# Modulations first in one run, half of their blocks in fp32, tokens in groups of three tiles; residual rows in eight pieces, output stores in halves; two loads of the neighbourhood stage moved

## The chip, the cores and the metric

One core of one Trainium2 chip runs the whole program. The metric is the device time of one execution in microseconds. Five engines work side by side: TensorE (PE; its weight loads, PEld, overlap its products), VectorE (DVE), ScalarE (ACT), GpSimd (POOL) and SyncE (SP), which here does nothing but issue DMAs. Each engine runs its instructions in a fixed order and waits on semaphores for what others make. Transfers issued by one engine stand in its instruction order too: a DMA whose wait isn't met holds up those behind it.

## What is computed

Two layers of a diffusion backbone work on 1024 latent tokens (a grid of 16 rows by 64 columns) and 128 prompt tokens, 1024 features each. Layer 0 mixes tokens by latent attention with 16 heads, layer 1 by neighbourhood attention with 16 heads over the grid. Around both stands the same frame, cut here to what the change touches:

```python
for i in range(DEPTH):                                   # 2
    sh_p, sc_p, g_p = modulation(c_ctx, w_ada[i], b_ada[i])   # split(silu(cond) @ w + b, 3)
    sh_s, sc_s, g_s = modulation(c, w_ada[i], b_ada[i])
    hp = rms_norm(xp, pre_norm_g[i]) * (1.0 + sc_p) + sh_p
    hs = rms_norm(xs, pre_norm_g[i]) * (1.0 + sc_s[:, None]) + sh_s[:, None]
    ...                                                  # op, osm: the mixer and its output projection
    xp = xp + g_p * rms_norm(op, post_norm_g[i])
    xs = xs + g_s[:, None] * rms_norm(osm, post_norm_g[i])
```

All tensors are fp32. The kernel keeps the precision by splitting an operand into two fp32r parts (high: the rounded value, low: the rest) and adding three products of the parts (`mm3`, line 84).

## The kernel before

**Staging.** Tokens come in nine tiles of 128 rows: tiles 0 to 7 latent, tile 8 prompt. Weights come by SP into a ring of raw buffers and are split by ACT (high part, a cast) and DVE or POOL (low part, a subtraction) (`load_w`, `split_to`).

**The opening (lines 162 to 298).** Layer 0 needs two modulation vectors before any token can be built: s = 1 (scale) and s = 0 (shift). For each, `modulation_steps` goes through eight blocks of `w_ada` (128 x 1024, 512 KB): load into one of four raw buffers, split, and four products of 512 columns (two column halves, high and low part) with a stationary operand of four columns: the conditioning vectors' high and low parts. `modulation_cols` then turns the rows into columns by small fp32 products (line 183). The program's order is: modulation 1, load and normalise x tiles 0 to 3, modulation 0, gate weights of head 0, x tiles 4 to 7, build the transposed normalised tokens `hT` for tiles 0 to 3, gate weights of head 1, x tile 8, normalise tiles 4 to 8, build 4 to 7, build 8. `norm_x` works tile by tile: two squares on ACT, then seven small instructions on DVE with a square root on ACT between, and one scaling. `build_ko` transposes a block of columns on PE (line 236), applies scale and shift (even blocks on DVE, odd ones on ACT) and splits. The gates of heads 0 and 1 follow as products over three groups of 384 tokens each (`proj_group`, line 395; `gate`, line 431).

```python
for _ in modulations(0, (1,)): pass
load_x(range(0, 4)); norm_x(range(0, 4))
for _ in modulations(0, (0,)): pass
```

**Order of the work.** A planner orders the instructions of each engine in the opening by their place in the program and by times that it reckons; SP is ordered by it throughout. `tc.issue_after(ins)` puts what is traced in its block behind `ins` on that engine. From the attention loop on, and again from line 1723 to the end, the orders of PE, ACT, DVE and POOL are those written out by hand.

**The neighbourhood stage (lines 1714 to 1811).** 64 units (8 head pairs, 4 column groups, 2 heads) run through a software pipeline, index k from -2 to 63; `NORDER` lists the steps of one k. `pair_proj` projects queries and keys of a head pair; `put_k` writes keys and copies them by DMA to the other half of the partitions (line 1440; `last_k` is the last of these). `windows(p, cg)` loads the values of a column group, five DMAs (lines 1567 and 1570), into one of two buffers, once for two units. `out_load` loads gated rows of an output tile into a raw buffer and notes them for a split; `last_split` does the split that is noted. In one k the step `W` does one piece of the output weights, which also splits what is noted.

**The tail (lines 1812 to 1820).** For each of nine output tiles PE makes 48 products of 512 columns (`out_steps`). `out_norm` loads the tile's residual rows and calls `post_norm`: squares on ACT, scaling by the gate row on DVE (line 1140), inverse root, then per half one `scalar_tensor_tensor` that adds the residual (line 1144), then one store of the whole tile. Because a tile here is 8 grid rows by 16 grid columns, its residual rows come in four DMAs of 32 rows, each two runs of 16 rows in DRAM:

```python
src = [x1_d[4 * rg + q].rearrange("(r c) f -> r c f", c=GW)[:, 16 * cg:16 * cg + 16, :] for q in range(4)]
return [(xr[32 * q:32 * q + 32, :], src[q]) for q in range(4)]
```

The buffers for residual rows and for results (`nq0`, `nq1`) are two each.

Of the kernel before, what the change touches and what calls it, by code (L numbers as in the profile page):

```python
# [3 lines left out]

# [1 line left out]

# [5 lines left out]
F32 = mybir.dt.float32  # L12
F32R = mybir.dt.float32r
AF = mybir.ActivationFunctionType
# [42 lines left out]
def hybrid_step(ctx: ExitStack, tc: tile.TileContext, i, o):  # L57
# [103 lines left out]

    def modulation_steps(l, s, ring):

        mod5 = pg.tile([5, D], F32, tag="mod5", name="mod5", bufs=1)
        dma(mod5[4:5, :], i["b_ada"][l:l + 1, s * D:(s + 1) * D])
        pm = [bank("M"), bank("M")]
        for k in range(NKO):
            w2 = load_w(ring, i["w_ada"][l, k * P:(k + 1) * P, s * D:(s + 1) * D], 2, 4, V,
                        lambda: pg.tile([P, 1024], F32, tag="raw", name="w_raw", bufs=4))
            for n in range(2):  # L170
                for e, w in enumerate(w2):
                    nc.tensor.matmul(pm[n][0:4, :], cs[:, k, :], w[:, n * 512:(n + 1) * 512],
                                     start=k == 0 and e == 0, stop=k == NKO - 1 and e == 1)
# [80 lines left out]
    ph1 = es_h1.enter_context(tc.tile_pool(name="ph1", bufs=1))  # L254
    hT = [ph1.tile([P, NKO, NTOK], F32R, name=f"hT{e}") for e in range(2)]
    pg = es_h1.enter_context(tc.tile_pool(name="pg", bufs=1, reuse_waits="tile"))

    def modulations(l, ss, ring=pg):
        for s in ss:
# [10 lines left out]
    def load_x(ts):  # L270
        with tc.issue_after(last_load[0]):
            for t in ts:
                last_load[0] = dma(xt[t], i["xs"][t * P:(t + 1) * P, :] if t < NLT else i["xp"]).ins

    def norm_x(ts):
        for t in ts:
            r = row_rstd(xpool, halves(xt[t]))
            V.tensor_scalar(xt[t], xt[t], r[:, 0:1], None, ALU.mult)

    for _ in modulations(0, (1,)):  # L280
        pass
    def build_h0(w, t0, n):
        build_h(0, w, lambda ko: xpool.tile([P, 512], F32, tag="htmp", name="htmp", bufs=3), xt[t0:t0 + n],
                lambda e, ko: hT[e][:, ko, t0 * P:(t0 + n) * P])

    load_x(range(0, 4))
    norm_x(range(0, 4))
    for _ in modulations(0, (0,)):
        pass
    gw = [gate_w(0)]  # L290
    load_x(range(4, 8))
    build_h0(0, 0, 4)
    gw.append(gate_w(1))
    load_x([8])
    norm_x(range(4, NT))
    build_h0(0, 4, 4)
    build_h0(1, 8, 1)
    es_x.close()

    es1 = ExitStack()  # L300
# [94 lines left out]
    def proj_group(w, src, g, evac, tag):  # L395

        ps = bank(tag)[:, :384]
        for ko in range(NKO):
            mm3(ps, [w[e][:, ko * P:(ko + 1) * P] for e in range(2)], [src(e, ko, g) for e in range(2)],
                ko == 0, ko == NKO - 1)  # L400
        evac(g, ps)

    def load_head(h, tile_):

        raw, rr = tile_[:, 0:512], None
# [22 lines left out]
        split_to(wv[0], wv[1], raw[:, 384:512])  # L428
        head_wv[h] = wv

    def gate(h, w, tag="S"):
        def evac(g, ps):
            gt = pg.tile([P, 384], F32, tag="gt", name="gt", bufs=3)
            S.activation(gt, ps, AF.Silu)
            dma(gate_d[h][:, g * 384:(g + 1) * 384], gt)
        for g in range(3):
            proj_group(w, lambda e, ko, g: hT[e][:, ko, g * 384:(g + 1) * 384], g, evac, tag)
            yield

    gates = [gate(h, w) for h, w in enumerate(gw)]  # L440
    for _ in zip(*gates):
        pass
    narrow(0)
    for h in range(2, 6):
        for _ in gate(h, gate_w(h)):
# [684 lines left out]
    for _ in rest:  # L1130
        pass

    def post_norm(pool, xr, parts, x_src, gp, dst, *junk_ring):

        for d, sr in x_src(xr):
            dma(d, sr)  # L1136

        def scaled():
            for x, c0, n in parts:
                V.tensor_tensor(dst[:, c0:c0 + n], x, gp[:, c0:c0 + n], ALU.mult)  # L1140
        r = row_rstd(pool, [x for x, _, _ in parts], scaled, *junk_ring)
        for _, c0, n in parts:
            c = slice(c0, c0 + n)
            V.scalar_tensor_tensor(dst[:, c], dst[:, c], r[:, 0:1], xr[:, c], ALU.mult, ALU.add)

    gpt = [t4(f"gpt{w}") for w in range(2)]
    for w in range(2):
# [394 lines left out]
                ko == 0, ko == 7)  # L1542
            yield

    def out_norm(t):
        parts = [(ps, hf * 512, 512) for hf, ps in enumerate(outs[t])]
        cg, rg = t // 2, t % 2

        def x1_rows(xr):
            if t == NLT:  # L1550
                return [(xr, x1_d[8])]
            src = [x1_d[4 * rg + q].rearrange("(r c) f -> r c f", c=GW)[:, 16 * cg:16 * cg + 16, :] for q in range(4)]
            return [(xr[32 * q:32 * q + 32, :], src[q]) for q in range(4)]
        xr, y = [p5.tile([P, NTOK], F32, tag=x, name=f"xy_{x}", bufs=2)[:, 0:D] for x in ("nq0", "nq1")]
        post_norm(p5, xr, parts, x1_rows, gpu[0 if t < NLT else 1], y, ("pf", 5))
        if t < NLT:
            dst = o["ys"].rearrange("(r c) f -> r c f", c=GW)
            dma(dst[8 * rg:8 * rg + 8, 16 * cg:16 * cg + 16, :], y)
        else:
            dma(o["yp"], y)  # L1560

    ogs, outs = {}, {}

# [179 lines left out]
    for k in range(-2, N):  # L1743
# [14 lines left out]
        if k == N - 2:  # L1758
# [8 lines left out]
        for step in NORDER.split():  # L1767
# [15 lines left out]
            elif c == "h":  # L1783
                on(na_hi, k + 1, int(n))
            elif c == "l":
                on(na_lo, k + 1, int(n))
            elif c == "E":
                on(na_values, k)
            elif c in "fg" and k >= 0:
                it = its[k]  # L1790
                na_out(it["po"], it["e"], 256, "fg".index(c))
                if it["e"] == 1 and c == "g":
                    gt = pairs[it["p"]]["gt"]
                    na_gate(it["p"], grid(gt)[:, :, 16 * it["cg"]:16 * it["cg"] + 16],
                            (2 * it["cg"], 2 * it["cg"] + 1), 256)
            elif c == "J":
                for _ in range(int(n) + (k < 0)):
                    next(proj, None)
            elif c == "K" and later:
                later.popleft()()  # L1800
            elif c == "X" and k >= N - 8:
                for _ in range(int(n)):
                    if n_out < 14 or k > N - 2:
                        next(out, None)
                        n_out += 1
            elif c == "W":
                (slow.popleft() if slow else last_split)()
# [116 lines left out]
```

## Time and profile before

| | |
|---|---|
| median of three runs | 2196.53 us (2195.59 to 2197.91) |
| the profiled execution's own time | 2195.93 us |
| its span in the trace | 2194.1 us |
| PE busy | 2016.6 us, 92% of the span |
| DVE, ACT, POOL busy | 1474.7, 1113.5, 850.0 us |
| moved by DMA | 256.49 MB, mean 117 GB/s |

The span runs from the first to the last instruction; the execution's own time has 1.8 us more around it. Times in the trace count from the span's start. A matmul's end is modelled, so a busy PE isn't PE at its peak. The granted clock (PEclk) is a share of 2.4 GHz; 0.5 is 1.2 GHz.

### The profile page before, as it was taken

The page shows a single profiled execution, that of the slowest core. Times are in us where ns is not written, and L with a number is a line of the kernel's source. Part 1 is how long each engine was busy: PE and PEld are TensorE (multiplying, and loading weights), DVE is VectorE, ACT ScalarE, POOL GpSimd, SP SyncE. Part 2 cuts the span into 40 slices and gives each one's busy share as a digit, 9 for nine tenths or more (in the row PEclk, how much of TensorE's full clock was granted, in tenths as well). Part 3 has the DMA queues.
Part 4 walks back from the last instruction along what each step waited for, and adds up shares of the span by engine and source line. Part 5 has one row for each costly group of instructions (what it writes and reads, how often), then busy time and mean ns, then how long its engine had stood idle before and what let it go on. Part 6 is the DMA issues. An engine that isn't in the chain of part 4 may idle for free.

```text
span 2194.1 us, 37839 instructions
## 1 busy us (share of the span) xinstructions
PE 2016.6 (92%) x13166; PEld 1864.7 (85%) x13166; DVE 1474.7 (67%) x3258; ACT 1113.5 (51%) x2582; POOL 850.0 (39%) x843
## 2 busy tenths in 40 slices
PE   6999998989999898889897799999998999998995
PEld 2899998888888888889897688889888999998784
DVE  6723887778888878787887744542215888887742
ACT  7545115555656566656564433343114667666621
POOL 0412215666777667766764500010001333333300
PEclk8999999999999999999999999999999999999898
DMA  7223752212221213121212733335324555566632
GB/s 285 86 79 109 233 168 67 58 45 63 55 65 44 75 34 91 51 77 32 69 40 77 238 125 120 113 106 187 133 104 138 170 179 179 174 186 208 202 123 85
DMA packets 172740, 256.49 MB, mean 117 GB/s; under 512 B 19651, under 2 KB 137187, under 8 KB 172549
## 3 DMA queue, kind: packets, MB, share of 16 engines
q1 hardware_dynamic: 172420, 253.96, 37.2%
q8 instruction: 104, 1.70, 0.3%
q14 instruction: 88, 0.71, 0.1%
q0 software_dynamic: 128, 0.11, 0.0%
HBM read 182.58 MB, written 51.49 MB: 107 GB/s over the span
## 4 chain that ended last, share of the span: by engine, by line
PE 35%; DMA 7%; DVE 4%; ACT 3%; POOL 2%; issue 2%; SPq 1%; DVEq 0%; POOLq 0%; ACTq 0%
PE ps_S L87 14%; PE ps_W L87 8%; DMA xy_nq<-x_d 4%; PE ps_M L87 4%; PE ps_M L1643 2%; PE ps_T L1618 2%; PE ps_S L1591 1%; PE ps_S L1592 1%; POOL sm L796 1%; DMA w_raw<-in_wout 1%; ACT pf L775 1%; DVE og L82 1%; DMA w_raw<-og_d 1%; SPq L1136 1%; DMA nk<-nk 1%
## 5 line engine op out<-in xcount | busy, mean ns | idle before, releaser
L785 DVE TENSOR_TENSOR pT<-pf,pT 128x512 fp32r<-128x512 f32 (+1 forms) x320 | 308.7, 969 | 24.0 <-ACT pT L780 23.9
L796 POOL TENSOR_TENSOR sm<-sm,pf 128x512 f32<-128x512 f32 (+1 forms) x192 | 258.9, 1348 | 15.9 <-ACT pf L775 1.7
L87 PE MATMUL ps_M<-pT,cK 128*128 128x256 f32 x1728 | 259.3, 296 | 1.3 <-DVE pT L785 1.3
L87 PE MATMUL ps_W<-h,w 128*128 128x384 f32 x1152 | 239.5, 347 | 0.0
L87 PEld LDWEIGHTS ps_M<-pT,cK 128*128 128x128 f32 x1728 | 230.9, 198 | 1.9 <-DVE pT L785 1.9
L87 PEld LDWEIGHTS ps_W<-h,w 128*128 128x128 f32 x1152 | 200.3, 190 | 5.7
L717 PE MATMUL ps_S<-qA,cKT 128*128 128x256 f32 x1152 | 190.8, 285 | 5.1 <-ACT pf L775 4.7
L87 PE MATMUL ps_S<-hT,w_hi 128*128 128x384 f32 x720 | 188.3, 339 | 4.8 <-DVE hT L82 3.8
L780 ACT CAST pT<-pf 128x512 fp32r<-128x512 f32 (+1 forms) x320 | 179.8, 591 | 0.0
L717 PEld LDWEIGHTS ps_S<-qA,cKT 128*128 128x128 f32 x1152 | 166.6, 192 | 7.6 <-ACT pf L775 7.0
L1613 POOL TENSOR_SCALAR pf<-pf,li 128x512 f32<-128x512 f32 x128 | 91.0, 711 | 204.1 <-DVE li L1610 178.2
L87 PEld LDWEIGHTS ps_S<-hT,w_hi 128*128 128x128 f32 x720 | 130.6, 189 | 6.8 <-DVE hT L82 4.9
L793 POOL TENSOR_TENSOR sm<-pf 128x512 f32<-128x512 f32 x64 | 88.9, 1389 | 108.8 <-ACT pf L775 108.4
L87 PE MATMUL ps_S<-wo,og 128*128 128x512 f32 x432 | 124.9, 397 | 0.0
L762 ACT CAST q<-ps_M 2x256 fp32r<-2x256 f32 x63 | 22.8, 362 | 197.1 <-PE ps_M L756 193.0
L87 PE MATMUL ps_S<-hT,w_lo 128*128 128x384 f32 x360 | 121.2, 337 | 0.0
L1607 ACT ACTIVATE pf<-pf,nm 128x512 f32<-128x512 f32 x128 | 93.0, 727 | 39.6 <-DVE nm L1604 36.2
L775 ACT ACTIVATE pf<-ps_S 128x512 f32<-128x512 f32 x192 | 108.9, 598 | 0.2 <-PE ps_S L768 0.2
L717 PE MATMUL ps_S<-q,KR 128*128 128x256 f32 x384 | 108.7, 284 | 0.4 <-DMA q<-w_raw 0.4
L82 DVE TENSOR_TENSOR og<-w_raw,og 128x512 fp32r<-128x512 f32 x56 | 57.1, 1042 | 67.9 <-ACT og L148 67.9
L495 ACT COPY qt<-ps_W 128x384 f32<-128x384 f32 (+1 forms) x104 | 47.0, 452 | 101.0 <-PE ps_W L87 92.4
L717 PE MATMUL ps_T<-qA,cKT 128*128 128x256 f32 x576 | 97.3, 284 | 0.0
(363 smaller groups left out, 5053.8 us busy)
## 6 DMA issues: line engine op xcount, KB each, us to landing
w_raw<-in_w_ada SPq DMA_DIRECT2D x48, 512.0 KB
w_raw<-og_d SPq DMA_DIRECT2D x41, 512.0 KB
vw<-vd SPq DMA_DIRECT2D x128, 128.0 KB
bias<-in_bias SPq DMA_DIRECT2D x64, 192.0 KB
q<-rp SPq DMA_DIRECT2D x126, 96.0 KB
gate_d<-gt SPq DMA_DIRECT2D x48, 192.0 KB
w_raw<-in_wgate SPq DMA_DIRECT2D x16, 512.0 KB
gt<-gate_d SPq DMA_DIRECT2D x64, 128.0 KB
```

Source lines behind the costliest of these rows:

```text
L82: eng.tensor_tensor(out, a, b, ALU.subtract)
L87: nc.tensor.matmul(ps, lhs[a], rhs[b], start=first and n == 0, stop=last and n == 2)
L495: (eng.copy if eng is S else eng.tensor_copy)(out, src)
L717: nc.tensor.matmul(ps[:, c:c + 256], k_[:, j, :], q_[:, un["qs"]], start=c == 0 and n == 0, stop=n == 3, skip_group_check=True)
L775: S.activation(pf, un["banks"][b][:, :w], AF.Exp)
L780: S.copy(un["pT"][b][0][:, :pf.shape[1]], pf)
L785: V.tensor_tensor(x[1], pf, x[0].bitcast(F32), ALU.subtract)
L793: G.tensor_tensor(un["sm"], un["pf"][0], pf, ALU.add)
L796: G.tensor_tensor(sm[:, :w], sm[:, :w], pf, ALU.add)
L1607: S.activation(it["pf", rg], it["pf", rg], AF.Exp, bias=it["nm", rg], scale=1.0, accum_out=it["li", rg])
L1613: G.tensor_scalar(it["pf", rg], it["pf", rg], it["li", rg][:, 0:1], 1.0, ALU.mult, ALU.mult)
L1618: nc.tensor.transpose(pt[:, j * P:(j + 1) * P], it["pf", rg][:, j * P:(j + 1) * P], ident)
```

## The change

- Opening: both modulations run one after the other in one loop, s = 1 first; s = 0 uses other PSUM banks (S) than s = 1 (M). Of the eight blocks of each, the odd ones aren't split: the raw fp32 block is multiplied in fp32 by `c0`, a new four-column operand that holds the conditioning vectors themselves and zeros (two products in place of four).
- x tiles 0 to 2 are loaded behind blocks 3 to 5 of the first modulation and normalised as a group; tiles 3 to 5 are loaded behind the gate weights of head 0, tiles 6 to 8 behind those of head 1. `norm_x` does its small instructions once for a group of three.
- For each group of three tiles in turn: normalise (groups 1 and 2), build, and the products of that group for the gates of heads 0 and 1. `proj_group` and `gate` move up in the text for this and stay as they were.
- Neighbourhood stage: the window loads traced at k < 2 are issued behind the last key copy; the first load of gated rows stands at the end of step N-13 in place of the start of step N-12; the immediate split at N-11 is left out.
- Tail: the residual rows of the next tile are loaded before a tile's normalisation is traced, in eight DMAs of 16 rows, each one run in DRAM; the store goes in two column halves, each behind its add; the very last half is issued by ACT.

```diff
@@ modulation_steps
-        pm = [bank("M"), bank("M")]
+        pm = [bank("SM"[s]), bank("SM"[s])]
         for k in range(NKO):
-            w2 = load_w(ring, i["w_ada"][l, k * P:(k + 1) * P, s * D:(s + 1) * D], 2, 4, V,
-                        lambda: pg.tile([P, 1024], F32, tag="raw", name="w_raw", bufs=4))
+            src = i["w_ada"][l, k * P:(k + 1) * P, s * D:(s + 1) * D]
+            new = lambda: pg.tile([P, 1024], F32, tag="raw", name="w_raw", bufs=4)
+            if k % 2:
+                raw = new()
+                last_load[0] = dma(raw, src).ins
+                parts = [(c0[:, k, :], raw)]
+            else:
+                parts = [(cs[:, k, :], w) for w in load_w(ring, src, 2, 4, V, new)]
             for n in range(2):
-                for e, w in enumerate(w2):
-                    nc.tensor.matmul(pm[n][0:4, :], cs[:, k, :], w[:, n * 512:(n + 1) * 512],
-                                     start=k == 0 and e == 0, stop=k == NKO - 1 and e == 1)
+                for e, (c, w) in enumerate(parts):
+                    nc.tensor.matmul(pm[n][0:4, :], c, w[:, n * 512:(n + 1) * 512],
+                                     start=k == 0 and e == 0, stop=k == NKO - 1 and e == len(parts) - 1)
             yield
...
+    c0 = pg.tile([P, NKO, 4], F32, name="c0")
+    V.memset(c0, 0.0)
+    for w in range(2):
+        V.tensor_copy(c0[:, :, 2 * w], cs_f[:, :, 2 * w])
@@ norm_x
     def norm_x(ts):
-        for t in ts:
-            r = row_rstd(xpool, halves(xt[t]))
-            V.tensor_scalar(xt[t], xt[t], r[:, 0:1], None, ALU.mult)
+        ss = xpool.tile([P, 3, 2], F32, tag="ssx", name="ss", bufs=2)
+        for k, t in enumerate(ts):
+            for hf, x in enumerate(halves(xt[t])):
+                junk = xpool.tile([P, 512], F32, tag="ntmp", name="junk", bufs=1)
+                S.activation(junk, x, AF.Square, accum_out=ss[:, k, hf:hf + 1])
+        s1 = xpool.tile([P, 3], F32, tag="ss_3", name="ss_3", bufs=2)
+        V.tensor_reduce(s1, ss, AX.X, ALU.add)
+        V.tensor_scalar(s1, s1, 1.0 / D, EPS, ALU.mult, ALU.add)
+        r = rsqrt(xpool, s1, 3)
+        for k, t in enumerate(ts):
+            V.tensor_scalar(xt[t], xt[t], r[:, k:k + 1], None, ALU.mult)
@@ the opening
-    for _ in modulations(0, (1,)):
-        pass
-    load_x(range(0, 4))
-    norm_x(range(0, 4))
-    for _ in modulations(0, (0,)):
-        pass
+    for n, _ in enumerate(modulations(0, (1, 0))):
+        if n in (3, 4, 5):
+            load_x(n - 3)
+        if n == 5:
+            norm_x(range(0, 3))
     gw = [gate_w(0)]
-    load_x(range(4, 8))
-    build_h0(0, 0, 4)
+    for t in range(3, 6):
+        load_x(t)
     gw.append(gate_w(1))
-    load_x([8])
-    norm_x(range(4, NT))
-    build_h0(0, 4, 4)
-    build_h0(1, 8, 1)
+    for t in range(6, NT):
+        load_x(t)
...
+    gates = [gate(h, w) for h, w in enumerate(gw)]
+    for g in range(3):
+        if g:
+            norm_x(range(3 * g, 3 * g + 3))
+        build_h0(0, 3 * g, 3 if g < 2 else 2)
+        if g == 2:
+            build_h0(1, 8, 1)
+        for x in gates:
+            next(x)
...
-    gates = [gate(h, w) for h, w in enumerate(gw)]
-    for _ in zip(*gates):
-        pass
     narrow(0)
@@ post_norm
-    def post_norm(pool, xr, parts, x_src, gp, dst, *junk_ring):
-        for d, sr in x_src(xr):
+    def post_norm(pool, xr, parts, x_src, gp, dst, *junk_ring, put=None):
+        for d, sr in x_src(xr) if x_src else ():
             dma(d, sr)
...
             V.scalar_tensor_tensor(dst[:, c], dst[:, c], r[:, 0:1], xr[:, c], ALU.mult, ALU.add)
+            if put:
+                put(c)
@@ out_norm
+    def out_x(t):
+        cg, rg = t // 2, t % 2
+        xr = p5.tile([P, NTOK], F32, tag="nq0", name="xy_nq0", bufs=2)[:, 0:D]
+        if t == NLT:
+            dma(xr, x1_d[8])
+            return xr
+        for r in range(8):
+            row = r % 2 * GW + 16 * cg
+            dma(xr[16 * r:16 * r + 16, :], x1_d[4 * rg + r // 2][row:row + 16, :])
+        return xr
-    def out_norm(t):
+    def out_norm(t, xr, last):
...
-        post_norm(p5, xr, parts, x1_rows, gpu[0 if t < NLT else 1], y, ("pf", 5))
-        if t < NLT:
+        y = p5.tile([P, NTOK], F32, tag="nq1", name="xy_nq1", bufs=2)[:, 0:D]
+        def put(c):
             dst = o["ys"].rearrange("(r c) f -> r c f", c=GW)
-            dma(dst[8 * rg:8 * rg + 8, 16 * cg:16 * cg + 16, :], y)
-        else:
-            dma(o["yp"], y)
+            dst = o["yp"][:, c] if t == NLT else dst[8 * rg:8 * rg + 8, 16 * cg:16 * cg + 16, c]
+            (nc.scalar.dma_start if last and c.start else dma)(dst, y[:, c])
+        post_norm(p5, xr, parts, None, gpu[0 if t < NLT else 1], y, "pf", 5, put=put)
@@ the neighbourhood loop
-            it["vw"] = windows(it["p"], it["cg"]) if it["e"] == 0 else its[k]["vw"]
+            with tc.issue_after(last_k[0]) if k < 2 else nullcontext():
+                it["vw"] = windows(it["p"], it["cg"]) if it["e"] == 0 else its[k]["vw"]
-        if k in (N - 12 + 1, N - 3, N - 1):
+        if k in (N - 3, N - 1):
             last_split()
-        if k == N - 12:
-            out_load(order[0], slice(0, 7))
...
+        if k == N - 13:
+            out_load(order[0], slice(0, 7))
@@ the tail
+    xr = out_x(order[0])
     for n, t in enumerate(order):
         for _ in out:
             pass
-        out_norm(t)
+        xr, nxt = (out_x(order[n + 1]) if n + 1 < NT else None), xr
+        out_norm(t, nxt, n + 1 == NT)
```

## Rows read from the trace of the kernel before

**Rows 1.** The page, part 1: busy us (share of the span) and instructions.

```profile
PE 2016.6 (92%) x13166; PEld 1864.7 (85%) x13166; DVE 1474.7 (67%) x3258; ACT 1113.5 (51%) x2582; POOL 850.0 (39%) x843
```

**Rows 2.** Windows: from:to, length, busy us (instructions) of each engine, PEclk, DMA share, GB/s.

```profile
20.00:25.00 5.00, 2.71 (x18) 2.02 (x18) 1.49 (x10) 4.83 (x11) 0.00 (x0) 1.00 1.03 420
...
25.00:30.00 5.00, 1.13 (x3) 0.18 (x4) 4.50 (x21) 4.68 (x14) 0.00 (x0) 0.51 0.40 161
...
43.00:80.00 37.00, 31.18 (x168) 28.43 (x169) 33.13 (x69) 25.76 (x59) 19.45 (x15) 0.86 0.59 191
...
80.00:320.00 240.00, 238.54 (x1377) 232.99 (x1376) 143.38 (x279) 89.56 (x199) 47.30 (x40) 1.00 0.43 134
...
2130.00:2144.00 14.00, 14.00 (x63) 11.45 (x62) 5.03 (x12) 2.53 (x6) 0.00 (x0) 1.00 0.31 114
```

**Rows 3.** Timeline of the opening: start us, us, engine line op [idle before].

```profile
6.97 1.01 PE L172 MATMUL ps_M<-w_hi,cs 128*4 128x512 f32 x2 [6.97 <-ACT w_hi L148]
...
20.40 0.62 PE L172 MATMUL ps_M<-w_lo,cs 128*4 128x512 f32 x2 [0.64 <-DVE w_lo L82]
...
28.63 1.02 PE L172 MATMUL ps_M<-w_hi,cs 128*4 128x512 f32 x2 [5.04 <-ACT w_hi L148]
...
42.18 0.63 PE L172 MATMUL ps_M<-w_lo,cs 128*4 128x512 f32 x2
...
48.56 0.81 DVE L245 TENSOR_SCALAR htmp<-ps_T,acol,shcol 128x512 f32<-128x512 f32 x1
...
80.14 1.03 PE L236 MATMUL ps_T<-ident,x 128*128 128x128 f32 x8
```

**Rows 4.** Line 183's instructions: count, duration ns min/median/max, first and last start.

```profile
L183 PE MATMUL ps_T<-sel,mod x32: 246/246/369, 21.4 to 47.4; 5*128 5x2 f32 x32
```

**Rows 5.** Timeline, entry of the neighbourhood stage.

```profile
1657.11 4.34 SPq L1570 DMA_DIRECT2D vw<-vd  x3
...
1661.56 1.47 SPq L1440 DMA_DIRECT2D nk<-nk  x2
...
1663.91 1.43 DVE L82 TENSOR_TENSOR w<-w_raw,w 128x256 fp32r<-128x256 f32 x4
...
1668.01 0.77 PE L1591 MATMUL ps_S<-nk,nq 128*128 128x512 f32 x1 [5.50 <-DMA nk<-nk]
...
1669.00 7.57 PE L87 MATMUL ps_W<-h,w 128*128 128x384 f32 x30
...
1689.47 1.26 PE L1643 MATMUL ps_M<-pT,vw 128*128 128x256 f32 x10
```

**Rows 6.** Timeline, late in the neighbourhood stage.

```profile
2024.49 1.03 ACT L1514 CAST w<-w_raw 128x512 fp32r<-128x512 f32 x2 [4.58 <-DMA w_raw<-og_d]
...
2027.83 2.37 PE L1618 MATMUL ps_T<-ident,pf 128*128 128x128 f32 x8 [5.04 <-POOL pf L1613]
```

**Rows 7.** Timeline of the tail.

```profile
2087.73 4.38 SPq L1136 DMA_DIRECT2D xy_nq<-x_d  x4
...
2092.13 11.31 PE L87 MATMUL ps_W<-nwo,w 128*128 128x512 f32 x48
...
2095.31 1.42 DVE L1144 SCALAR_TENSOR_TENSOR xy_nq<-xy_nq,rs_y,xy_nq 128x512 f32<-128x512 f32 x2
...
2134.03 9.79 SPq L1136 DMA_DIRECT2D xy_nq<-x_d  x4
...
2136.51 11.31 PE L87 MATMUL ps_W<-nwo,w 128*128 128x512 f32 x48
...
2147.82 8.59 SPq L1136 DMA_DIRECT2D xy_nq<-x_d  x4
...
2163.03 10.95 PE L87 MATMUL ps_W<-nwo,w 128*128 128x512 f32 x46 [0.52 <-DVE w L82]
...
2185.81 1.41 DVE L1144 SCALAR_TENSOR_TENSOR xy_nq<-xy_nq,rs_y,xy_nq 128x512 f32<-128x512 f32 x2 [7.37 <-DMA xy_nq<-x_d]
```

**Rows 8.** Line 229's instructions, columns as in rows 4.

```profile
L229 SPq DMA_DIRECT2D gp_d<-mg x2: 379/379/379, 248.1 to 324.6; - x2
```

More of the change, by code (lines that the diff above doesn't have):

```diff
@@ L2 @@
 from collections import deque, namedtuple
-from contextlib import ExitStack
+from contextlib import ExitStack, nullcontext
 import numpy as np
@@ L268, in hybrid_step, with proj_group, load_x @@
     xt = [xpool.tile([P, D], F32, name=f"x{t}") for t in range(NT)]
-    def load_x(ts):
+    def proj_group(w, src, g, evac, tag):
+        ps = bank(tag)[:, :384]
+        for ko in range(NKO):
+            mm3(ps, [w[e][:, ko * P:(ko + 1) * P] for e in range(2)], [src(e, ko, g) for e in range(2)],
+                ko == 0, ko == NKO - 1)
+        evac(g, ps)
+    def load_x(t):
         with tc.issue_after(last_load[0]):
-            for t in ts:
-                last_load[0] = dma(xt[t], i["xs"][t * P:(t + 1) * P, :] if t < NLT else i["xp"]).ins
+            last_load[0] = dma(xt[t], i["xs"][t * P:(t + 1) * P, :] if t < NLT else i["xp"]).ins
     def norm_x(ts):
-        for t in ts:
-            r = row_rstd(xpool, halves(xt[t]))
-            V.tensor_scalar(xt[t], xt[t], r[:, 0:1], None, ALU.mult)
-    for _ in modulations(0, (1,)):
-        pass
+        ss = xpool.tile([P, 3, 2], F32, tag="ssx", name="ss", bufs=2)
[9 more added lines that the diff above has]
+            V.tensor_scalar(xt[t], xt[t], r[:, k:k + 1], None, ALU.mult)
     def build_h0(w, t0, n):
@@ L284, in build_h0, with gate, evac @@
                 lambda e, ko: hT[e][:, ko, t0 * P:(t0 + n) * P])
-    load_x(range(0, 4))
-    norm_x(range(0, 4))
-    for _ in modulations(0, (0,)):
-        pass
+    for n, _ in enumerate(modulations(0, (1, 0))):
[3 more added lines that the diff above has]
+            norm_x(range(0, 3))
     gw = [gate_w(0)]
-    load_x(range(4, 8))
-    build_h0(0, 0, 4)
+    for t in range(3, 6):
+        load_x(t)
     gw.append(gate_w(1))
-    load_x([8])
-    norm_x(range(4, NT))
-    build_h0(0, 4, 4)
-    build_h0(1, 8, 1)
+    for t in range(6, NT):
+        load_x(t)
+    def gate(h, w, tag="S"):
+        def evac(g, ps):
+            gt = pg.tile([P, 384], F32, tag="gt", name="gt", bufs=3)
+            S.activation(gt, ps, AF.Silu)
+            dma(gate_d[h][:, g * 384:(g + 1) * 384], gt)
+        for g in range(3):
+            proj_group(w, lambda e, ko, g: hT[e][:, ko, g * 384:(g + 1) * 384], g, evac, tag)
+            yield
+    gates = [gate(h, w) for h, w in enumerate(gw)]
+    for g in range(3):
+        if g:
[5 more added lines that the diff above has]
+            next(x)
     es_x.close()
@@ L393, in narrow @@
         put_kr(j, pt[:, 3 * P:4 * P])
[L395 to L401, printed above, removed]
     def load_head(h, tile_):
@@ L429, in split_v @@
         head_wv[h] = wv
[L431 to L438, printed above, removed]
-    gates = [gate(h, w) for h, w in enumerate(gw)]
-    for _ in zip(*gates):
-        pass
     narrow(0)
@@ L1140, in scaled @@
                 V.tensor_tensor(dst[:, c0:c0 + n], x, gp[:, c0:c0 + n], ALU.mult)
-        r = row_rstd(pool, [x for x, _, _ in parts], scaled, *junk_ring)
+        r = row_rstd(pool, [x for x, _, _ in parts], scaled, *([junk_ring] if junk_ring else []))
         for _, c0, n in parts:
@@ L1543, in out_steps @@
             yield
-    def out_norm(t):
+    def out_x(t):
[9 more added lines that the diff above has]
+    def out_norm(t, xr, last):
         parts = [(ps, hf * 512, 512) for hf, ps in enumerate(outs[t])]
         cg, rg = t // 2, t % 2
[L1549 to L1554, printed above, removed]
-        post_norm(p5, xr, parts, x1_rows, gpu[0 if t < NLT else 1], y, ("pf", 5))
-        if t < NLT:
+        y = p5.tile([P, NTOK], F32, tag="nq1", name="xy_nq1", bufs=2)[:, 0:D]
+        def put(c):
             dst = o["ys"].rearrange("(r c) f -> r c f", c=GW)
-            dma(dst[8 * rg:8 * rg + 8, 16 * cg:16 * cg + 16, :], y)
-        else:
-            dma(o["yp"], y)
+            dst = o["yp"][:, c] if t == NLT else dst[8 * rg:8 * rg + 8, 16 * cg:16 * cg + 16, c]
+            (nc.scalar.dma_start if last and c.start else dma)(dst, y[:, c])
+        post_norm(p5, xr, parts, None, gpu[0 if t < NLT else 1], y, "pf", 5, put=put)
     ogs, outs = {}, {}
```

## The prediction

> **What bounds the kernel now.** I read the page's first part first: TensorE (PE) is busy for 92% of the span [rows 1], so PE decides, except in stretches where it stands still. The windows show where that is [rows 2]. From 80 to 320 us PE is busy 238.54 of 240 us at 2.4 GHz, so a stretch of work that starts earlier there also ends earlier. Before it stands an opening in which PE waits: 25 to 30 us holds 1.13 us of PE work, and from 43 to 80 us VectorE (DVE) is the fuller engine, 33.13 of 37 us against PE's 31.18 with a granted clock of 0.86. At the other end, 2130 to 2144 us, PE is full, but the transfers move only 114 GB/s at a DMA share of 0.31, while 420 GB/s were possible at 20 to 25 us.
>
> The timeline of the opening [rows 3] has the two modulations that the first normalised rows need: the first from 6.97 to 21.0 us, the second from 28.63 to 42.8 us. Between them the reader sees 7.6 us without a modulation matmul: ScalarE (ACT) and DVE normalise four row tiles, whose instructions stand ahead of the second modulation's splits. The first build instruction comes at 48.56 us.
>
> At the entry of the neighbourhood stage [rows 5] PE waits 5.50 us, to 1668.01, for key copies that SP issued only at 1661.56, behind three window loads whose issuing took from 1657.11 to 1661.5. Late in that stage [rows 6] a PE wait of 5.04 us follows a ScalarE cast that stood 4.58 us for a load of gated rows. In the tail [rows 7] the output products take 11.1 us a tile ((2136.51 - 2092.13) / 4 groups), but the residual rows come ever later: issuing the four pieces of a tile grows from 4.38 to 9.79 us, and the last add waits 7.37 us and starts at 2185.81. (The chain of waits ends there too: the add, and before it these transfers, tile after tile.)
>
> **The opening.** A block of 512 KB now costs four products of 512 columns: 11.31 us for 48 [rows 7], so 0.232 us each at 2.4 GHz and 0.93 us a block. Half of the blocks (8 of 16) become two fp32 products. Their price isn't in the trace. The low end is the same 0.232 us. The high end comes from fp32 rows: eight transposes of 128 columns take 1.03 us [rows 3], 0.109 us apart, so 0.43 us for 512 columns, and line 183's 16 fp32 products stand as 32 records [rows 4], two for each: 0.87 us. I take 0.87, the nearer kind. A block is then 1.74 us, and PE has 8 x 0.81 = 6.5 us more to do. ACT is spared 8 casts, DVE as many subtractions.
>
> A pair of blocks is thus 2.67 us of PE, 21.4 us for all 16; at today's pace (14.1 us for 8) it would be 28.3 us. With the start at 6.97 the second modulation ends between 28.4 and 35.3 us, if the hole of 7.6 us goes; it goes because both modulations now follow each other in every queue and only six row squares stand among their casts. Later than 42.8 us it ends only if PE stays at 1.2 GHz: 42.7 us of products, end at 49.7. Its first matmuls do run at half speed (two in 1.01 us against 0.62 later). I take 33.5 us, near today's pace, because four raw buffers still carry the blocks and three row tiles are loaded among them: 9.3 us gained.
>
> The Trainium skill (FP8 and Floating Point Precision, section "TensorE Precision Notes") speaks against this half of the change: true FP32 goes through the array in four passes. By that, an estimate of 4 x 0.232 = 0.93 us a product, PE would have 7.4 us more in place of 6.5; no row here times such a product, and the 9.3 us would shrink by at most 0.9.
>
> What is late next: DVE. Three groups of three tiles need as many built columns as two of four and one; the small norm instructions come once for a group and not for a tile, which spares DVE some. The two gates' products start with the first three tiles. I give this 0.7 us and 10 us for the whole opening. Its ends: 7 us lost (PE at 1.2 GHz), 16 us gained (28.4 us and a fuller PE afterwards). The moved x loads (nine, each now behind a weight load on SP) stand before PE's first need, at the cost of ACT and DVE stalls where they don't, inside these ends. The shift is carried by the full PE from 80 us on.
>
> **The two neighbourhood loads.** The windows of the first two units go behind the key copies on SP. The copies are then issued when ACT has written the keys, about 1658.5 us, with no window ahead. But PE can't go on at once: the projection of the next pair needs weight splits that DVE does from 1663.91 on (four in 1.43 us), so the first is there at about 1664.3. PE's 30 products at 1669.00 [rows 5] then come 4.7 us earlier. They took 7.57 us; at 0.232 x 384/512 = 0.174 us each they would take 5.2: the wait had brought the clock down to 1.2 GHz, and I count half of the 2.4 us. Together 5.9 us; ends 0 (DVE late by as much) and 7.9. The windows themselves come later by up to 10 us, and the second ones wait for the next pair's first key copies; the first values product that reads a window stands at 1689.47, and that covers it. Without that cover their landing would be PE's wait.
>
> The load of gated rows moves from the start of one step to the end of the step before. Between the two stand only loads, no compute, and the buffer that it needs comes free at the same split, so the 4.58 us wait stays, in the main. One split that was done at once now goes in halves into free places. I take 1 us, with ends of 1 us lost and 7 us gained (the PE wait of 5.04 us and the slow products behind it gone).
>
> **The tail.** A tile's residual rows come now in four pieces of 32 rows, afterwards in eight of 16 rows, each one run of DRAM. Issuing: the 16-row DMA of the trace, line 229, takes 0.379 us [rows 8], so 3.0 us a tile, under the 11.1 us that PE needs. How fast such a piece lands no row shows. The ends are the full rows of the opening (420 GB/s, 512 KB in 1.25 us) and the 32-row pieces of today (four issued in 9.79 us). I take the fast end: what is slow today isn't the memory (share 0.31, 114 GB/s), and 16 rows of 4 KB have the form of the 128-row loads. The Trainium skill (DMA: Bandwidth & Descriptors, section "Why a DMA increments its semaphore by 16 and not by 1") has a rule for this: a DMA runs on the largest number of engines, up to 16, that divides the outermost size of both its sides. By it today's piece, two runs of DRAM, uses two engines, the new one 16, and the sum is as I make it; the share of 0.31 agrees, no view names the engines.
>
> With the rows in time PE keeps its 11.1 us: groups start at 2147.6 and 2158.7 and end at 2169.8, against 2163.03 + 10.95 = 2174.0 now. The add follows a PE end by 3.2 us where it doesn't wait (2095.31 against 2092.13), so 2173.0 in place of 2185.81: 12.8 us. The last store's second half leaves by ACT's queue behind a first half that is already moving; I take 0.8 us, with ends of 0.5 lost and 1.5 gained, by half of a 256 KB share. The earlier halves cost SP one more issue a tile, beside PE's products. Tail: 13.6 us. If a row piece is late now, it is the load of gated rows; it stands behind 3 us of issuing and has a tile's time.
>
> **Sum.** 10 + 5.9 + 1 + 13.6 = 30.5 us off the profiled execution's 2195.93 us (span 2194.1 and 1.8 around it): 2165.4. The median of the runs, 2196.53, is 0.6 us above it: 2166.
>
> **The rivals.**
> - The opening gains nothing: fp32 products at 1.2 GHz, or ACT and DVE unable to feed PE while they build (33 of 37 us busy speaks for it; fewer splits against). 2166 + 10 = 2176.
> - Some waits go altogether: the stall at 2027.83 too, and the opening gives 16 us. 2166 - 6 - 6 = 2154. For it: the load is traced earlier; against: its buffer isn't free earlier.
> - The row pieces stay as slow as today's, so the change doesn't do what it says there: the tail keeps all but the 0.8 us of the store. 2166 + 12.8 = 2179.
> - Slower: a 16-row piece is one run, today's has two. If the runs set how wide a piece is carried, eight pieces take twice 9.79 us, and with the rest of today's distance of 13.8 us (2147.82 - 2134.03), 4.0 us of stores and gated loads, a tile takes 23.6 us. Seven tiles from 2087.73 on end at 2253, and 8.3 us more for add and store (2194.1 - 2185.81) make 2261, 67 us later than now; with 17 us from the other edits 2196 + 67 - 17 = 2246. It decides once a tile's rows need more than PE's 11.1 us. By the skill's rule that happens if the instruction carries the source as one run without the rows; the 128-row loads, runs of the same length from contiguous DRAM, speak against it.
>
> **How the numbers follow.** Forecast 0.63, opening nothing 0.13, more waits gone 0.12, pieces as slow as today 0.05, slower 0.04, and 0.03 for the planned part between (its order is made anew) giving all of it back. Range 2153 to 2181: it takes in the first four cases and their unknown prices, and leaves out under 2 in 10. The forecast's own range is 2157 to 2175. 0.2%, 4.4 us, is about what a measurement of this kernel can tell from no change. Faster 0.93, within it 0.03, slower 0.04.
>
> **What would show it.** Right: no modulation gap near 21 to 28 us, fp32 products near 0.87 us, the first build instruction near 38 us; the key copies issued before 1660 less the shift and no PE wait of 5 us there; PE groups 11.1 us apart to the end and adds that wait for no residual rows. Wrong: modulation matmuls at half rate throughout, a new wait for windows in the first units, residual transfers of over 11 us.

## The result, and the profile after

The changed kernel takes 2179.68 us (median of four runs, 2177.92 to 2181.47), the kernel before beside it 2197.18: a ratio of 0.9921, interval 0.9904 to 0.9939. That is 17.5 us of the 30.5 forecast. The time lies inside the stated range (2153 to 2181), at its upper end, and outside the forecast's own (2157 to 2175). The profiled execution took 2177.92 us, 18.0 less than the one of before.

The page's first part; PE is no less busy than in [rows 1], it waits less:

```profile
PE 2017.5 (93%) x13166; PEld 1861.4 (86%) x13166; DVE 1460.2 (67%) x3224; ACT 1105.3 (51%) x2577; POOL 854.0 (39%) x847
```

Windows, columns as in [rows 2]:

```profile
25.00:30.00 5.00, 5.00 (x20) 1.59 (x19) 1.46 (x3) 1.92 (x3) 0.00 (x0) 1.00 0.81 267
...
43.00:80.00 37.00, 33.03 (x177) 29.42 (x176) 30.93 (x61) 25.86 (x57) 19.80 (x17) 0.91 0.47 152
80.00:320.00 240.00, 236.68 (x1350) 230.34 (x1350) 141.57 (x274) 88.54 (x200) 51.68 (x42) 1.00 0.42 134
...
2130.00:2144.00 14.00, 14.00 (x62) 11.36 (x61) 4.95 (x12) 3.18 (x8) 0.00 (x0) 1.00 0.48 144
```

The hole at 25 to 30 us is filled, but from 80 to 320 us PE now has fewer records than before (1350 against 1377) and 3.3 us without work against 1.5. The timeline of the opening shows the rest:

```profile
6.64 1.01 PE L179 MATMUL ps_M<-w_hi,cs 128*4 128x512 f32 x2 [6.64 <-ACT w_hi L148]
...
13.10 1.88 PE L179 MATMUL ps_M<-w_raw,c 128*4 128x512 f32 x4
...
33.26 1.88 PE L179 MATMUL ps_S<-w_raw,c 128*4 128x512 f32 x4 [1.04 <-DMA w_raw<-in_w_ada]
...
37.48 1.88 PE L179 MATMUL ps_S<-w_raw,c 128*4 128x512 f32 x4
...
42.48 0.68 DVE L252 TENSOR_SCALAR htmp<-ps_T,acol,shcol 128x384 f32<-128x384 f32 x1
...
68.73 0.44 PE L87 MATMUL ps_S<-hT,w_hi 128*128 128x384 f32 x1 [2.59 <-DVE hT L82]
...
103.72 0.62 PE L87 MATMUL ps_S<-hT,w_hi 128*128 128x384 f32 x2 [0.91 <-ACT gt L327]
...
105.05 0.62 PE L87 MATMUL ps_S<-hT,w_hi 128*128 128x384 f32 x2 [0.71 <-ACT gt L327]
```

Against [rows 3] the first build instruction is 6.1 us earlier (42.48 against 48.56), not 10, and then new PE waits follow. At the entry of the neighbourhood stage the key copies now stand ahead of the windows, and the wait of 5.50 us of [rows 5] is gone; a shorter one for a later pair's copies is new:

```profile
1653.48 6.13 SPq L1466 DMA_DIRECT2D nk<-nk  x4
1659.66 0.58 SPq L1599 DMA_DIRECT2D vw<-vc_d  x1
1660.29 2.31 SPq L1602 DMA_DIRECT2D vw<-vd  x4
...
1664.63 5.15 PE L87 MATMUL ps_W<-h,w 128*128 128x384 f32 x28 [0.43 <-DVE w L82]
...
1717.15 0.48 PE L1623 MATMUL ps_S<-nk,nq 128*128 128x512 f32 x1 [1.31 <-DMA nk<-nk]
```

Late in the stage both waits of [rows 6] stay, and weight loads are waited for behind them:

```profile
2017.94 1.03 ACT L1540 CAST w<-w_raw 128x512 fp32r<-128x512 f32 x2 [4.30 <-DMA w_raw<-og_d]
...
2021.28 2.37 PE L1650 MATMUL ps_T<-ident,pf 128*128 128x128 f32 x8 [4.43 <-POOL pf L1645]
...
2037.23 1.05 ACT L148 CAST nwo<-w_raw 128x1024 fp32r<-128x1024 f32 x1 [1.80 <-DMA w_raw<-in_nwout]
...
2041.24 0.66 PE L1650 MATMUL ps_T<-ident,pf 128*128 128x128 f32 x4 [1.66 <-POOL pf L1645]
```

The tail, to be held against [rows 7]: PE groups 11.0 to 11.2 us apart, eight pieces issued in 5 us, no add waits for rows:

```profile
2120.89 11.20 PE L87 MATMUL ps_S<-nwo,w 128*128 128x512 f32 x48
...
2126.39 4.99 SPq L1580 DMA_DIRECT2D xy_nq<-x_d  x8
...
2131.93 11.31 PE L87 MATMUL ps_W<-nwo,w 128*128 128x512 f32 x48
...
2135.30 1.42 DVE L1168 SCALAR_TENSOR_TENSOR xy_nq<-xy_nq,rs_y,xy_nq 128x512 f32<-128x512 f32 x2 [0.24 <-DVE rs_y L128]
...
2168.63 1.41 DVE L1168 SCALAR_TENSOR_TENSOR xy_nq<-xy_nq,rs_y,xy_nq 128x512 f32<-128x512 f32 x2 [0.24 <-DVE rs_y L128]
2170.07 1.22 ACTq L1591 DMA_DIRECT2D out_ys<-xy_nq  x1
```

To say where the 18.0 us came from, I paired every PE product of the two traces with its counterpart and read how much earlier it starts ("shift" below; negative is later). It is 0.2 us at 316 us and -0.2 at 1640; 6.8 at 1690, 5.2 at 1730; 4.6 at 2080; the rest comes behind. So, in this pair: opening -0.2 (with all that this one execution lost or won up to 1640), entry +5.5 (7.0 less 1.5), from there through the late load -0.7, tail +13.4.

### The profile page after: what moved, and what is told of

The parts are those of the page before. It is cut to its first block, busy times and chain, and to the rows that moved or that the text cites. A ratio compares the mean times of both kernels' runs of the same rounds, so it can differ in the third digit from the quotient of the medians.

```text
span 2176.1 us, 37859 instructions
## 1 busy us (share of the span) xinstructions
PE 2017.5 (93%) x13166; PEld 1861.4 (86%) x13166; DVE 1460.2 (67%) x3224; ACT 1105.3 (51%) x2577; POOL 854.0 (39%) x847
## 4 chain that ended last, share of the span: by engine, by line
PE 40%; DVE 4%; ACT 4%; POOL 4%; DMA 3%; issue 2%; SPq 0%; DVEq 0%; POOLq 0%; ACTq 0%
PE ps_S L87 16%; PE ps_W L87 11%; PE ps_M L87 5%; PE ps_M L1675 2%; POOL sm L820 2%; PE ps_T L1650 2%; PE ps_S L1623 1%; PE ps_S L1624 1%; ACT pf L799 1%; DMA vw<-vd 1%; DMA w_raw<-in_wout 1%; DVE rm L754 1%; DVE pT L809 1%; DVE og L82 1%; DMA w_raw<-og_d 1%
```

## The experiments

**Each part alone, in the kernel before.**

```diff
# e_open: only the hunks of modulation_steps, c0, norm_x, the opening, proj_group and gate
# e_entry: only
+            with tc.issue_after(last_k[0]) if k < 2 else nullcontext():
# e_late: only the load at N-13 in place of N-12, and (N - 3, N - 1)
# e_tail: only the hunks of post_norm, out_x, out_norm and the tail's loop
```

> The kernel before with the opening part alone (modulations in one run, half of the blocks in fp32, tokens in three groups). Theory A, from the two traces: the part starts the first build 6 us earlier, but the PE waits that come between 63 and 113 us and slower products up to 320 us give all of it back, so the time stays within 1.5 us of before (2196 to 2198) and the products over hT between 120 and 316 us stand 175 ns apart (median) against 173 before. Theory B, the forecast: 10 us are gained at the opening and carried to the end, 2187; in the changed kernel they were then lost to something outside the opening.

> The kernel before with only the windows of the first two units issued behind the last key copy. Theory A, from the traces: 7.0 us gained at 1668, 1.5 us given back at about 1717 by a new wait for a later pair's key copies, so 5.5 us, 2191.5. Theory B, the forecast without that new wait: 5.9 us by another sum, 2191. Rival: the order that SP's planner makes for the rest of the stage is other without the other parts, and the wait at 1717 is absent: 7 us, 2190.

> The kernel before with only the first load of gated rows at the end of the step before, and the immediate split left out. Theory A, from the traces: the load's wait of 4.6 us stays, and the split in halves costs waits for the gated probabilities behind it, 0.7 us lost, 2198. Theory B, the forecast: 1 us gained, 2196. Rival: the stall at 2028 goes altogether, 7 us gained, 2190.

> The kernel before with only the tail (residual rows a tile ahead in eight pieces of 16 rows, stores in halves, the last by ACT). Theory A and the forecast: PE groups 11.1 us apart, 12.6 us before the last add and 0.8 us behind it, 13.4 us, 2183.5. Rival: part of the tail's gain came with the shift of the rest (the loads of the first tiles come earlier against the last window loads), then under 11 us alone, over 2186.

Ratios to before, with the gain in us of its 2198.57 in these rounds:

| part | ratio, interval | gain | forecast |
|---|---|---|---|
| opening | 0.9977 (0.9968 to 0.9986) | 5.1 | 10 |
| entry | 0.9969 (0.9958 to 0.9980) | 6.8 | 5.9 |
| late load | 1.0025 (1.0015 to 1.0035) | -5.5 | 1 |
| tail | 0.9946 (0.9934 to 0.9958) | 11.9 | 13.6 |

The sum is 18.3 us, the whole change gives 17.4 by its ratio: with intervals of about 2 us either way for each part, the parts add. The opening lies between my two theories. The entry's 2192.25 us can't tell its three figures (2190 to 2191.5) apart; its trace gains 7.0 us and gives 4.1 back at 1717. The tail's 2186.46 us lies over the 2186 of its rival, and its interval (9.2 to 14.5 us) holds both. Its trace decides for theory A: it had lost 3.1 us by 2080 us, and its last add is still 9.5 us earlier than before (2185.81), so 12.6 us were gained behind:

```profile
2176.32 1.41 DVE L1144 SCALAR_TENSOR_TENSOR xy_nq<-xy_nq,rs_y,xy_nq 128x512 f32<-128x512 f32 x2 [0.24 <-DVE rs_y L128]
```

The late load was expected at 2198 or less and took 2204.66: the sign of theory A, but eight times its size; the profile of the changed kernel alone had hidden it. First the place in the kernel before, then in e_late:

```profile
2030.85 1.80 SPq L1497 DMA_DIRECT2D w_raw<-in_nwout  x2
...
2041.44 1.04 ACT L148 CAST nwo<-w_raw 128x1024 fp32r<-128x1024 f32 x1
```


```profile
2031.88 1.14 ACT L1514 CAST nwo<-w_raw 128x512 fp32r<-128x512 f32 x2
...
2033.65 0.34 SPq L1497 DMA_DIRECT2D w_raw<-in_nwout  x1
...
2039.85 0.33 SPq L1497 DMA_DIRECT2D w_raw<-in_nwout  x1
...
2046.65 1.05 ACT L148 CAST nwo<-w_raw 128x1024 fp32r<-128x1024 f32 x1 [2.94 <-DMA w_raw<-in_nwout]
...
2050.67 0.66 PE L1618 MATMUL ps_T<-ident,pf 128*128 128x128 f32 x4 [2.80 <-POOL pf L1613]
```

The reader is to see two weight loads issued together before and 6.2 us apart now, then ScalarE standing 2.94 us for the second and PE 2.80 us behind it. The split at N-11 used to be done whole, and its buffer was free at once. In halves, DVE's two subtractions come at 2035.55 and 2037.42, the buffer is free at 2038.1, and three window issues, from 2037.82 to 2039.6, then stand ahead of the load.

**Which half of the late edit.** In the changed kernel: both halves put back (b_nolate), and only the split (b_keep).

```diff
-        if k in (N - 3, N - 1):
+        if k in (N - 12 + 1, N - 3, N - 1):
# b_nolate also has the load at N-12 again
```

> The changed kernel with the late load of gated rows and the split of step N-11 put back as before; opening, windows and tail as changed. Theory A (that edit alone loses 4 to 6 us, as it did in the kernel before): 2174 to 2176, and the shift of PE against the kernel before doesn't fall between 2040 and 2055 us, where it fell by 2.7 us in the profiled changed kernel. Theory B (only the 0.7 us net that the changed kernel's own profile shows): 2179.

> The changed kernel with the load of gated rows moved as in the change, but the split of step N-11 done at once as before. Theory A (the split in halves frees its raw buffer late, the second weight load is issued some 4 us later, and ScalarE and then PE wait for it): the loss is gone, within 1.5 us of the kernel that has both put back, 2174 to 2176. Theory B (the moved load is what costs): within 1.5 us of the changed kernel, 2178.5 to 2181.

Ratios 0.9910 (0.9893 to 0.9926), 2178.08 us, and 0.9903 (0.9889 to 0.9917), 2176.81 us: each a little below the changed kernel, neither apart from it by its interval. Both miss the 2174 to 2176 of their theories A. b_nolate lies nearer to theory B; b_keep lies below its theory B and within 1.5 us of b_nolate, as its theory A asks. The trace of b_keep does show the step:

```profile
2024.08 1.04 ACT L148 CAST nwo<-w_raw 128x1024 fp32r<-128x1024 f32 x1
2025.84 1.80 SPq L1523 DMA_DIRECT2D w_raw<-in_nwout  x2
...
2036.71 1.05 ACT L148 CAST nwo<-w_raw 128x1024 fp32r<-128x1024 f32 x1
```

Both loads are issued together again, and the second cast waits for nothing. Between 1990 and 2080 us the six kernels with the whole edit lose 1.2 to 4.3 us of shift (mean 2.6), b_keep 0.5, the five without it -1.0 to 2.1 (mean 0.4; 2.1 is b_nolate itself, by a longer window wait at 2071). So the split in halves costs some 2 us by the traces and 3.3 to 7.7 by the timed runs in the kernel before; the moved load alone gave nothing that shows. That the whole edit costs time is shown by the timed runs; that the split in halves is what costs, by the traces alone; the size stays open.

**The tail: shape of the pieces or a tile ahead.** Both in the changed kernel.

```diff
# e_p32: four pieces of 32 rows, a tile ahead
+        for q in range(4):
+            src = x1_d[4 * rg + q].rearrange("(r c) f -> r c f", c=GW)[:, 16 * cg:16 * cg + 16, :]
+            dma(xr[32 * q:32 * q + 32, :], src)
# e_noahead: eight pieces of 16 rows, not ahead
+        out_norm(t, out_x(t), n + 1 == NT)
```

> The changed kernel with the residual rows in four pieces of 32 rows (two runs each) as before, still loaded a tile ahead. Theory A (the shape of the piece sets the pace, order alone doesn't cure it): issuing four pieces still takes 8 to 10 us a tile, but a tile ahead they have 11.1 us, so most of the adds are in time and the last add comes 0 to 4 us later than in the changed kernel: 2180 to 2184. Theory B (the pieces of 32 rows hold back the stores and the loads of gated rows behind them on SP, and these become the bound): PE groups stay over 12.5 us apart and the tail's gain is lost, 2190 to 2193.

> The changed kernel with the eight pieces of 16 rows issued where the loads stood before, at the start of the tile's own normalisation, not a tile ahead. Theory A (the shape alone suffices): a tile's rows land within 6 us of the issue, before the add needs them; PE groups 11.1 us apart, time within 1.5 us of the changed kernel, 2178 to 2181. Theory B (being a tile ahead is what cures it): adds wait several us each and the last add comes 5 us or more later, over 2185.

e_p32: 0.9963 (0.9951 to 0.9975), 2189.63 us, 0.4 below the range of theory B and far over that of theory A; e_noahead: 0.9906 (0.9892 to 0.9921), 2176.72 us, 1.3 below the range of theory A, and theory B falls. First e_p32's trace, then e_noahead's:

```profile
2148.58 8.25 SPq L1580 DMA_DIRECT2D xy_nq<-x_d  x4
2157.72 1.41 DVE L1168 SCALAR_TENSOR_TENSOR xy_nq<-xy_nq,rs_y,xy_nq 128x512 f32<-128x512 f32 x2 [7.33 <-DMA xy_nq<-x_d]
...
2171.57 1.41 DVE L1168 SCALAR_TENSOR_TENSOR xy_nq<-xy_nq,rs_y,xy_nq 128x512 f32<-128x512 f32 x2 [7.32 <-DMA xy_nq<-x_d]
...
2184.16 1.41 DVE L1168 SCALAR_TENSOR_TENSOR xy_nq<-xy_nq,rs_y,xy_nq 128x512 f32<-128x512 f32 x2 [7.38 <-DMA xy_nq<-x_d]
```

```profile
2146.45 4.96 SPq L1580 DMA_DIRECT2D xy_nq<-x_d  x8
...
2154.98 1.41 DVE L1168 SCALAR_TENSOR_TENSOR xy_nq<-xy_nq,rs_y,xy_nq 128x512 f32<-128x512 f32 x2 [0.24 <-DVE rs_y L128]
```

With pieces of two runs the adds wait 7.3 us even a tile ahead; with pieces of one run none waits, though nothing is traced ahead. And the adds of e_p32 follow each other by 13.9 and 12.6 us, in the pace of the kernel before (13.7 and 12.6):

```profile
2159.57 1.41 DVE L1144 SCALAR_TENSOR_TENSOR xy_nq<-xy_nq,rs_y,xy_nq 128x512 f32<-128x512 f32 x2 [7.46 <-DMA xy_nq<-x_d]
...
2173.22 1.41 DVE L1144 SCALAR_TENSOR_TENSOR xy_nq<-xy_nq,rs_y,xy_nq 128x512 f32<-128x512 f32 x2 [7.31 <-DMA xy_nq<-x_d]
```

So the pieces of 32 rows set the tail's pace themselves, wherever they stand. Theory B of e_p32 came near the number, but put the bound on what stands behind the pieces; the last add waits for the pieces. By the traces the tail gains 1.4 us with them in place of 13.4, by the medians the old shape takes back 10 of 12; being a tile ahead adds nothing that shows. Whether the two runs or the 32 rows of a piece make it slow, no run here takes apart.

**The opening: fp32 blocks, and where c0 lies.** Both in the changed kernel.

```diff
# e_split: all sixteen blocks through load_w
-            if k % 2:
+            if False:
# o_c0x: c0 out of the weight ring's pool
-    c0 = pg.tile([P, NKO, 4], F32, name="c0")
+    c0 = xpool.tile([P, NKO, 4], F32, name="c0")
```

> The changed kernel with all sixteen modulation blocks split (no fp32 products), the rest as changed. Theory A (the opening's end is set after the modulations, by the build and the gates): the second modulation ends at another time, 37 to 42 us, but at 125 us and at the end the time is the same within 1.5 us, 2178 to 2181. Theory B (PE's 6.5 us of fp32 products cost what the opening should have gained): without them the time is 4 to 6 us shorter, 2174 to 2176. Theory C (ACT and DVE bound the opening, as the change assumes): all split is 3 to 7 us slower, 2183 to 2187.

> The changed kernel with the new four-column fp32 operand c0 allocated in the pool of the token tiles, so that the ring of weight buffers lies at the addresses that it had before (c0 moved them by 128 bytes a partition). Theory A (the slower products between 120 and 320 us come from where the weights lie): products over hT stand 173 ns apart again, the shift of 1.4 us at 125 us stays until 320, 1.2 us gained, 2178.5. Theory B (they come from something else, the order or the traffic): median 175 ns and no gain, 2179.7.

e_split: 0.9923 (0.9909 to 0.9936), 2179.89 us; o_c0x: 0.9918 (0.9904 to 0.9931), 2178.89 us. Neither time tells from the changed kernel; the traces do. For the table I added up what PE's instructions behind the second modulation's last product take at 2.4 GHz ("work"). It says how many us earlier than the kernel before each kernel has done so much work:

| work done, us | 10 | 20 | 30 | 50 | 60 | 100 |
|---|---|---|---|---|---|---|
| reached before at | 57.1 | 72.3 | 83.2 | 103.3 | 114.4 | 154.8 |
| changed kernel | 5.7 | 9.0 | 5.5 | 3.8 | 1.7 | 1.4 |
| e_split | 6.4 | 10.2 | 9.3 | 6.9 | 6.3 | 6.0 |
| b_best (below) | 4.4 | 8.3 | 7.3 | 4.9 | 4.3 | 4.5 |

The seven kernels with the opening as changed reach the last column -1.4 to 3.7 us earlier, mean 1.2; the three all-split ones (the third is b_vw4, below) 4.5 to 6.0. So theory C falls: without fp32 products the second modulation ends earlier (37.97 against 39.36 us), although ACT and DVE split twice as many blocks. Theory A has the time (2178 to 2181), but its reason falls too: the work of 100 us is done 6.0 us earlier than before, against 1.4 in the changed kernel, a difference of 4.6 and not under 1.5. The traces bear out theory B's reason, and its time (2174 to 2176) is missed. All split, 4.2 of 10.2 us are still lost between work 20 and 100, so fp32 isn't the whole of it. No run takes the groups of three tiles apart from the single run of the modulations, and what each of them does there is not shown. That the total didn't follow is shown only in part: e_split's shift falls by 4.2 us at 490 and 545 us, where the granted clock of 8 us is 0.79 against 1.00 before (1.5 of it comes back at 534, where the kernel before has such a drop), and by 4.3 around the late load.

o_c0x allocates c0 elsewhere, so that the ring lies as before; c0 ahead of it had moved it by 128 bytes a partition. The same products between 125 and 310 us (columns: busy us, mean ns | idle), in the kernel before, the changed one, and o_c0x:

```profile
L87 PE MATMUL ps_S<-hT,w_hi 128*128 128x384 f32 x554 | 141.7, 336 | 0.0
```

```profile
L87 PE MATMUL ps_S<-hT,w_hi 128*128 128x384 f32 x548 | 141.7, 339 | 0.0
```

```profile
L87 PE MATMUL ps_S<-hT,w_hi 128*128 128x384 f32 x544 | 139.2, 336 | 0.0
```

From start to start the products over hT stand 173 ns apart (median; mean 173.6) in the four kernels with the opening as before, in o_c0x, and in the two of the last experiment, which have no c0; 175 (mean 176.0) in all seven with c0 ahead of the ring: theory A. 2.4 ns by some 820 products are 1.9 us, but the shift loses only about 0.7 us more than in o_c0x on this stretch. Why the address matters, no run shows.

**A version from these, and the lesson tried elsewhere.** b_best: all split, no c0, late load as before, windows and tail as changed. b_vw4: the same with the window loads cut to one run each.

```diff
# b_vw4
-            dma(vw[:, qd, :].bitcast(F32), src[:, COL0[cg]:COL0[cg] + 32, :])
+            for r in range(4):
+                dma(vw[32 * r:32 * r + 32, qd, :].bitcast(F32), src[r, COL0[cg]:COL0[cg] + 32, :])
```

> The changed kernel with all sixteen modulation blocks split, without the fp32 operand c0 (so the weight ring lies as before), and with the late load as before. Theory A (terms add: 5 us from the late load, 4.5 us from the products in fp32, 1.2 us from the addresses): 2169 to 2171. Theory B (what the opening gains is lost to the clock in the attention stage, as the timed runs of the all-split kernel suggest): as the kernel without the late load, 2174 to 2176.

> The kernel of the run before this one (all split, no c0, late load as before) with each window load of 128 rows, four runs of DRAM, cut into four loads of 32 rows, one run each, the lesson of the residual rows put to the windows. Theory A (shape: the window loads then leave no backlog, so the key copies, the gated rows and the windows that PE waits for land earlier): the waits at 1717, 2021, 2029 and 2073 us shrink, 3 to 7 us faster than that kernel. Theory B (SP: twelve more issues of 0.35 us for every two units, 4 us in about 12, delay biases and copies): slower by 5 us or more.

b_best: 0.9880 (0.9864 to 0.9896), 2173.18 us, apart from the changed kernel's interval, with the fastest median here; between its two theories. Against b_nolate (2178.08 us), which differs from it by the fp32 blocks and c0 alone, it is 4.9 us faster, but the two intervals overlap by 0.0003. b_vw4: 1.0266 (1.0251 to 1.0282), 2257.72 us, theory B and far worse than its 5 us. SP's window issues from 1700 to 1900 us (count: ns min/median/max), in b_best and in b_vw4:

```profile
L1593 SPq DMA_DIRECT2D vw<-vd x63: 507/524/799, 1703.4 to 1899.9; - x63
```

```profile
L1594 SPq DMA_DIRECT2D vw<-vd x209: 302/419/1546, 1699.9 to 1899.7; - x105
```

All SP issues of these 200 us summed take 125 us in b_best and 173 in b_vw4. PE waits 19.9 us for window loads between 1650 and 2100 us, against 1.1 in b_best. So what the new shape may have gained is lost; how much of the 85 us is issuing and how much the landing of the pieces, these runs don't take apart.

## Why the prediction held in time and not in its sum

**What held.** The time is in the range because the range had room for the rivals: four terms were summed, one was near (the tail), one was met at its spot and then partly lost (the entry), one gave half (the opening), one had the wrong sign (the late load). The tail: PE groups 11.1 us apart, the last add at 2168.63 where the shift of 4.6 us and the forecast's 12.8 ask for 2168.4, the store 0.8 us shorter (7.5 us from the add to the span's end, 8.3 before). Issuing eight pieces took 5.0 us and not the 3.0 taken, still under the 11.1. The reason given, the form of the piece, is what the two tail kernels show. It also agrees with the rule of the Trainium skill that was weighed there (DMA: Bandwidth & Descriptors, "Why a DMA increments its semaphore by 16 and not by 1"); no view here names the engines. The entry: 7.0 us gained at the spot (5.9 forecast). The windows that were moved back were covered, as "that covers it" says; later key copies weren't: they stand behind other windows, and 0.7 to 4.1 us are given back at 1717 in the ten kernels with that edit. The late stall stayed, as forecast.

**The step that failed: the opening's 10 us.** Three terms of it.
- "A pair of blocks is thus 2.67 us", 33.5 us for the end. The fp32 product was sized right: four records in 1.81 us to the next start, 0.90 us a product (0.87 taken). The Trainium skill's four passes (FP8 and Floating Point Precision, "TensorE Precision Notes") gave 0.93, and the trace is nearer to it. But sixteen blocks took 32.7 us: 22 us of products, 2.5 more at the start, where products take about twice as long (the first fp32 block 3.31 us, later ones 1.88), 2 us for the first modulation's columns, which now stand between the second's products, 4.9 us of waits for casts, subtractions and one load, and small gaps. 3.4 us were gained where 9.3 were forecast.
- "The shift is carried by the full PE from 80 us on." In the changed kernel PE isn't full there. Of 9.0 us at work 20, 3.5 go at 66 to 75 us (PE waits 2.59 us for the second group's hT, then runs with a granted clock of 0.68 from 70 to 75), 3.7 up to 113 (waits at 91.00, 101.77, 103.72 and 105.05, 2.6 us together, where the kernel before has one of 0.8 us; the rest in small gaps).
- Half of the blocks in fp32 was taken as a relief for ACT and DVE that costs PE little. All split reaches work 100 some 4 us sooner.

The rival "the opening gains nothing" (0.13) is the nearest to this, by its second condition, ACT and DVE unable to feed PE while they build. But nothing it isn't: in the timed runs the opening alone gives 3.1 to 7.0 us; the traces of seven kernels give 1.2 on average at 155 us, with a spread of 5 us from run to run. That difference I leave open.

**The wrong sign: the late load.** I gave the split in halves no price, only "free places"; the bound of 1 us lost was too narrow, 3.3 to 7.7 us were lost in the kernel before. What decides is the raw buffer: two of them carry all weights, and a later subtraction is a later load.

The rival whose figure fits, 2179 with slow pieces, is not what happened: that the time falls on it is chance.

## What to carry to other kernels

A shift gained early is worth only what the stretch behind it can carry (here the next 50 us): before counting it, read which engine feeds the next stage, and whether its order still has work to fill PE's waits. When a split is postponed, price the buffer that it frees, not the engine time. A DMA's shape can outweigh its place in the queue (2189.6 us against 2176.7 here), but cutting a load in four is paid at some 0.4 us an issue (the windows of b_vw4), so count the queue's issues first.

## What the runs showed of the hardware

- Moving the weight buffers by 128 bytes a partition changes 384-column fp32r products from 173.6 to 176.0 ns (mean of some 820); a small allocation ahead of a ring was not free here.
- The same wait may or may not bring the clock down. At 408 us PE waits 1.63 us in the kernel before and in e_entry, with the same code in that stage; behind it the windows differ (kernel before, then e_entry; the column before the DMA share is the granted clock):

```profile
408.00:416.00 8.00, 7.74 (x62) 7.48 (x63) 5.84 (x12) 7.21 (x17) 5.83 (x6) 1.00 0.58 141
```

```profile
408.00:416.00 8.00, 6.89 (x38) 6.84 (x39) 3.04 (x9) 5.34 (x14) 4.49 (x4) 0.63 0.59 155
```

It costs e_entry 2.7 us of shift. Such drops move single executions by up to 5 us between 400 and 600 us, so one trace of a whole kernel can't settle a part of 3 us.
